# 192 instead of 160 tokens gathered in a product-key expert layer, with the gathers begun in the one-hot stage

## The chip, the cores and the metric

The kernel runs on one core of one Trainium2 chip. The metric is device time in microseconds of one execution, the median of several runs. The core has five engines with a queue each: TensorE (PE, matmuls, with its weight loads as PEld), VectorE (DVE), ScalarE (ACT), GpSimd (POOL) and SyncE (SP), and 16 DMA engines that the queues of SP, ACT and POOL share.

## The reference, cut to what matters

One encoder layer over 512 tokens of width 2048. The first half (gated linear attention and dilated window attention) isn't touched by the change. The second half is a channel mixer that looks up 128 x 128 = 16384 single-neuron experts:

```
qry = (xt @ w_query).reshape(T, 8, 2, 128)
sc = einsum('thcd,hckd->thck', qry, sub_keys)
top_s, top_i = top_k(sc, 16)                  # per token, head and side
cand_s = top_s[:, :, 0, :, None] + top_s[:, :, 1, None, :]
best_s, best_pos = top_k(cand_s, 16)          # 16 experts per token and head
idx, gates = ..., softmax(best_s)
u = expert_down[idx];  act = gelu(einsum('tkd,td->tk', u, x))
out = einsum('tk,tkd->td', gates * act, expert_up[idx])
```

So each token uses 8 x 16 = 128 experts, each with one row of `expert_down` and one of `expert_up` (8 KB each).

## The kernel before, in words

The second half treats two groups of tokens in two ways. 352 tokens are **dense** (`DENSE`, lines 24 to 31): all 16384 experts are computed for them by matmuls, and the gates, zero for the experts that a token doesn't use, are multiplied in. The other 160 are **gathered** (`NG` = `NA` + `NB2` = 128 + 32): for them the rows of the experts used are fetched from DRAM by index and multiplied on VectorE. A batch of 128 tokens lies on the 128 partitions (`xn`), so one slot (a head's k-th expert) takes one indirect DMA of 128 rows, 128 of them for the down rows and 128 for the up rows. The 32 tokens lie four times over the partitions (`xb`), so 32 DMAs serve their 128 slots. Each such row tile, 1 MB, is fetched by POOL's queue (`fetch_rows`, three buffers, two ahead; line 1180), and VectorE does one operation on it: a product with a sum for the down rows (line 1194), a scaled addition for the up rows (line 1209).

The weights of the dense part come as 128 down blocks and 128 up loads of 1 MB on SP's queue. `Stream` splits each into two pieces, each piece into a high half (ScalarE, line 71) and a lo half (VectorE or POOL, line 79, after `add_down`), and each product is three fp32r matmuls (`mm3`, lines 120 to 122), whose moving operand has 352 columns.

The stages in question, each in program order:

- **Query projection** (`Scores`, 8 heads x 4 loads): six matmuls per weight tile, three over the dense and three over the gathered columns. Beside it VectorE and POOL do the top-k of the heads (`TopK`, in pieces that `pieces` hands out).
- **Tail**: 42 steps (`HEAD`) of three matmuls for the first of the `EARLY` = 3 down blocks, with the top-k of the last head for the dense tokens between them.
- **One-hot stage** (88 steps of four dense tokens): VectorE compares indices with an iota (e, line 1118) and multiplies by the gates (w, line 1121); TensorE multiplies the two one-hots into a gate matrix of all experts (line 1146), which goes to DRAM (`gt_d`). Between the steps a filler does the down products of `INSIDE` = 19 more blocks, whose lo pieces are POOL's. The last top-k pieces stand here, and at step 70 the indices of the gathered tokens are made (`gathered_slots`). Activations of the first 8 blocks stay in SBUF (`pre0` to `pre7`), those of 16 more go to DRAM (`pre_d`) by `pre_store`.
- **Dense stage**: two more early blocks, then 16 groups of eight blocks: the down products not yet done, gelu, gates, split (`Weighted`), and 16 up loads. `after` is called once per piece and lets `gather` advance in proportion to the steps. All gathering stands in this stage. The gates come back from DRAM every four blocks (`fetch_gates`, the first two on POOL's queue, ahead of the gathers).

Every engine takes its instructions in the order in which the program writes them; no scheduler reorders them.

## Time and profile before

| | |
|---|---|
| median of 3 runs | 3273.18 us (3270.42 to 3275.17) |
| the profiled execution | 3277.63 us, span 3275.9 us |
| TensorE busy | 3210.5 us, 98% |
| VectorE busy | 2370.4 us, 72% |
| ScalarE, POOL busy | 36%, 28% |
| moved by DMA | 774.37 MB, 236 GB/s over the span |

Busy is the time in which an engine has at least one instruction running. TensorE's matmuls overlap, so its pace is read from the distance of their starts and not from their durations. A row of the timeline gives start, duration, engine, line, operation, operands and shapes. A row of stretches gives, for each engine, its busy time and its number of instructions, then the granted TensorE clock (1.00 is 2.4 GHz), the busy share of the DMA engines and their rate.

### The profile page before, as it was taken

The page shows a single profiled execution, that of the slowest core. Times are in us where ns is not written, and L with a number is a line of the kernel's source. Part 1 is how long each engine was busy: PE and PEld are TensorE (multiplying, and loading weights), DVE is VectorE, ACT ScalarE, POOL GpSimd, SP SyncE. Part 2 cuts the span into 40 slices and gives each one's busy share as a digit, 9 for nine tenths or more (in the row PEclk, how much of TensorE's full clock was granted, in tenths as well). Part 3 has the DMA queues.
Part 4 walks back from the last instruction along what each step waited for, and adds up shares of the span by engine and source line. Part 5 has one row for each costly group of instructions (what it writes and reads, how often), then busy time and mean ns, then how long its engine had stood idle before and what let it go on. Part 6 is the DMA issues. An engine that isn't in the chain of part 4 may idle for free.

```text
span 3275.9 us, 47661 instructions
## 1 busy us (share of the span) xinstructions
PE 3210.5 (98%) x19090; PEld 3012.4 (92%) x19090; DVE 2370.4 (72%) x3754; ACT 1178.4 (36%) x1892; POOL 919.6 (28%) x714
## 2 busy tenths in 40 slices
PE   8999999999999989998999999999999999999999
PEld 6778887878899988988999999999999999999999
DVE  5544445464457779946888888888888888888886
ACT  4334344453323345643333332332332332333332
POOL 3112020201235555501323323223233333233331
PEclk9999999999999999999999999999999999999999
DMA  4222222224322234577898989899889898988996
GB/s 148 81 91 93 75 94 73 96 94 143 131 83 91 80 142 178 187 279 264 331 342 346 348 324 351 327 347 343 339 332 351 316 353 324 356 344 329 356 344 228
DMA packets 157229, 774.37 MB, mean 236 GB/s; under 512 B 13264, under 2 KB 64784, under 8 KB 70672
## 3 DMA queue, kind: packets, MB, share of 16 engines
q1 hardware_dynamic: 99744, 389.31, 33.9%
q0 software_dynamic: 48768, 348.73, 27.0%
q10 hardware_dynamic: 8496, 33.30, 2.6%
q8 instruction: 150, 2.46, 0.3%
q14 instruction: 71, 0.58, 0.0%
HBM read 733.79 MB, written 37.49 MB: 235 GB/s over the span
## 4 chain that ended last, share of the span: by engine, by line
PE 78%; DVE 12%; DMA 5%; issue 2%; ACT 2%; POOL 1%; DVEq 0%; ACTq 0%; SPq 0%; POOLq 0%
PE pj L122 17%; PE pj L120 17%; PE pj L121 17%; PE pa L122 7%; PE pa L120 7%; PE pa L121 7%; DMA wr16x<-in_downT_dram 2%; DVE e L1118 2%; DMA wr4x<-in_upT_dram 2%; DVE w L1121 2%; DVE wl2x L79 1%; PE pa L603 1%; PE pa L544 1%; DVE row L1194 1%; PE pj L1146 1%
## 5 line engine op out<-in xcount | busy, mean ns | idle before, releaser
L79 DVE TENSOR_TENSOR wl2x<-wr4x,wh2x 128x1024 fp32r<-128x1024 f32 x382 | 467.3, 1230 | 350.3 <-ACT wh2x L71 344.4
L122 PE MATMUL pj<-ah,wl2x 128*128 128x352 f32 x2048 | 667.6, 326 | 9.7 <-DVE wl2x L79 9.5
L120 PE MATMUL pj<-ah,wh2x 128*128 128x352 f32 x2048 | 664.3, 324 | 12.3 <-ACT wh2x L71 12.2
L121 PE MATMUL pj<-al,wh2x 128*128 128x352 f32 x2048 | 662.4, 323 | 1.0 <-DVE al L1243 1.0
L122 PE MATMUL pa<-yh,wl8x 128*128 128x352 f32 x2000 | 652.2, 326 | 10.8 <-POOL wl8x L79 8.9
L120 PE MATMUL pa<-yh,wh8x 128*128 128x352 f32 x2000 | 660.2, 330 | 0.6 <-ACT wh8x L71 0.6
L121 PE MATMUL pa<-yl,wh8x 128*128 128x352 f32 x2000 | 645.8, 323 | 0.0
L71 ACT CAST wh2x<-wr4x 128x1024 fp32r<-128x1024 f32 x382 | 396.8, 1048 | 661.0 <-DMA wr4x<-in_upT_dram 384.9
L1180 POOL DMA_INDIRECT row<-in_down_dram,idx x160 | 255.1, 1595 | 678.1 <-DVE ga L1194 674.3
L1180 POOL DMA_INDIRECT row<-in_up_dram,idx x160 | 272.2, 1701 | 579.4 <-DVE xn L1209 432.5
L122 PEld LDWEIGHTS pj<-ah,wl2x 128*128 128x128 f32 x2048 | 386.9, 189 | 18.1 <-DVE wl2x L79 15.7
L120 PEld LDWEIGHTS pj<-ah,wh2x 128*128 128x128 f32 x2048 | 386.5, 189 | 14.9 <-ACT wh2x L71 14.3
L121 PEld LDWEIGHTS pj<-al,wh2x 128*128 128x128 f32 x2048 | 387.8, 189 | 2.1 <-DVE al L1243 1.9
L122 PEld LDWEIGHTS pa<-yh,wl8x 128*128 128x128 f32 x2000 | 374.9, 187 | 13.6 <-POOL wl8x L79 10.4
L120 PEld LDWEIGHTS pa<-yh,wh8x 128*128 128x128 f32 x2000 | 377.2, 189 | 2.0 <-ACT wh8x L71 1.0
L121 PEld LDWEIGHTS pa<-yl,wh8x 128*128 128x128 f32 x2000 | 376.6, 188 | 0.0
L71 ACT CAST wh8x<-wr16x 128x1024 fp32r<-128x1024 f32 x256 | 267.1, 1046 | 200.9 <-DMA wr16x<-in_downT_dram 129.3
L79 DVE TENSOR_TENSOR wl8x<-wr16x,wh8x 128x1024 fp32r<-128x1024 f32 x212 | 258.8, 1223 | 95.4 <-ACT wh8x L71 95.4
L1209 DVE SCALAR_TENSOR_TENSOR xn<-row,ga,xn 128x2048 f32<-128x2048 f32 x127 | 298.0, 2347 | 0.1
L1194 DVE CUSTOM_DVE_ANT_0 row<-row,xn 128x2048 f32<-128x2048 f32 x128 | 292.6, 2286 | 0.0
L120 PE MATMUL pj<-wh2x,xh 128*128 128x512 f32 x704 | 284.1, 404 | 0.0
L121 PE MATMUL pj<-wl2x,xh 128*128 128x512 f32 x704 | 274.7, 390 | 1.2 <-DVE wl2x L79 1.2
(330 smaller groups left out, 4842.6 us busy)
## 6 DMA issues: line engine op xcount, KB each, us to landing
wr16x<-in_downT_dram SPq DMA_DIRECT2D x128, 1024.0 KB, 6.8
wr4x<-in_upT_dram SPq DMA_DIRECT2D x128, 1024.0 KB, 7.5
wr4x<-in_win_dram SPq DMA_DIRECT2D x47, 1024.0 KB, 4.9
gt_d<-gs ACTq DMA_DIRECT2D x11, 2048.0 KB, 7.1
g<-gt_d SPq DMA_DIRECT2D x30, 704.0 KB, 8.8
wr4x<-in_wout_dram SPq DMA_DIRECT2D x16, 1024.0 KB, 5.0
wr8x<-in_wq_dram SPq DMA_DIRECT2D x16, 1024.0 KB, 5.1
xt<-in_xT_dram POOLq DMA_DIRECT2D x4, 1024.0 KB, 6.5
```

The lines of the kernel that those rows point to most:

```text
L71: self.nc.scalar.copy(hi, t)
L79: self.lo_engine[n].tensor_tensor(lo, t, hi.bitcast(F32), op=OP.subtract)
L120: nc.tensor.matmul(out, sh, mh, start=first, stop=False)
L121: nc.tensor.matmul(out, sh, ml, start=False, stop=False)
L122: nc.tensor.matmul(out, sl, mh, start=False, stop=last)
L544: nc.tensor.matmul(sc[u], qt[:, h, t * 128:(t + 1) * 128], kt[:, h, :], start=True, stop=True)
L603: nc.tensor.matmul(oo, vv[:, kb, h * 128:(h + 1) * 128], pt[u][:, kb, :], start=kb == 0, stop=kb == NB - 1)
L1118: nc.vector.tensor_tensor(e, ij[:, :, ts].unsqueeze(2).to_broadcast([128, 2, 128, 4]), io4.unsqueeze(1).to_broadcast([128, 2, 128, 4]), op ...
L1121: nc.vector.tensor_tensor(w[:, 0], e[:, 0].rearrange("p k t -> p t k"), gd[:, ts].unsqueeze(2).to_broadcast([128, 4, 128]), op=OP.mult)
L1180: nc.gpsimd.indirect_dma_start(out=t, out_offset=None, in_=A["up" if up else "down"], in_offset=bass.IndirectOffsetOnAxis(ap=idx[b][:, k:k ...
L1194: nc.vector.tensor_tensor_reduce(t, t, x, 1.0, 0.0, OP.mult, OP.add, g[:, k:k + 1])
L1209: nc.vector.scalar_tensor_tensor(x, t, g[:, k:k + 1], x, op0=OP.mult, op1=OP.add)
```

## The change

- `NB2` goes from 32 to 64: 192 tokens are gathered, 320 are dense. The 64 tokens lie twice over the partitions (`PARTS` = 2), so their slots take 64 DMAs; with the other 128 that is 192 for the down and 192 for the up rows.
- The tail is 122 steps long (`EARLY` = 8). In it the top-k of the gathered tokens comes before that of the dense ones, and all top-k is done there. At step 84 the indices are made and the first two rows fetched. One lo piece of every other early block goes to VectorE.
- The one-hot stage has 80 steps and no top-k; every third step holds one gather (27), while `INSIDE` = 22 blocks fill it.
- All 32 early activations go to DRAM; the eight of each of the first four groups are loaded by SP's queue.
- The dense stage goes on with the gathers where the one-hot stage ended.

```diff
-NB2 = 32
+NB2 = 64
+PARTS = 128 // NB2
...
-    EARLY, INSIDE = 3, 19
+    EARLY, INSIDE = 8, 22
...
-        ws.add(A["downT"][e], 2, () if e >= EARLY + INSIDE else (nc.gpsimd, nc.gpsimd))
+        ws.add(A["downT"][e], 2, () if e >= EARLY + INSIDE else (nc.gpsimd, nc.gpsimd if e >= EARLY or e % 2 else None))
...
             def rest(self):
                 self.packed(sel_h, 256, 64)
-                self.packed(sel_q, 320, 32)
...
                 self.packed(sel_a, DENSE + NB2, 128)
-                self.packed(sel_b, DENSE, 32)
+                self.packed(sel_b, DENSE, NB2)
...
+        gathered = [0]
+
+        def gather_next():
+            gather(gathered[0])
+            gathered[0] += 1
...
         def pre_store():
-            e = len(pre)
-            kept = e < E
-            t = prep.tile([128, DENSE], F32, name=f"pre{e}" if kept else "spill", bufs=1 if kept else 2)
+            t = spill.tile([128, DENSE], F32, name="spill", bufs=2)
             nc.vector.tensor_tensor(t, banks.pop(0), rb2[:, :DENSE], op=OP.mult)
-            if not kept:
-                nc.scalar.dma_start(pre_d[e], t)
+            nc.scalar.dma_start(pre_d[len(pre)], t)
             pre.append(t)
...
-        HEAD = 42
+        HEAD = 16 * EARLY - 6
         for n in range(HEAD):
             next(tail)
             if n == 5:
-                assert len(todo) < 8
+                assert len(todo) < 12
                 pieces(len(todo))
+                scored.gathered()
+            if n == 7:
                 scored.whole()
-            if n in (6, 12, 18, 24):
+                scored.rest()
+            if n >= 9 and n % 6 == 3:
                 pieces(1)
-            if n == 14:
-                scored.rest()
-            if n == 16:
-                scored.gathered()
-            if n == 30:
-                pre_store()
-            if n == 36:
+            if n == 84:
+                gathered_slots()
+                fetch_rows(0)
+                fetch_rows(1)
+            if n == 106:
+                assert not todo
                 flush()
-            if n == 40:
+            if n == 112:
                 turned_sel(0)
                 turned_sel(1)
+                turned_part(sel_h, 256, 64)
+            if banks and n % 16 == 5:
+                pre_store()
...
             one_hots(n + 2)
-            if n % 4 == 1 and n < 64:
-                pieces(1)
-            if n in (20, 36, 52, 68):
-                flush()
-            if n == 38:
-                turned_part(sel_h, 256, 64)
-            if n == 40:
-                turned_part(sel_q, 320, 32)
+            if n % 3 == 1:
+                gather_next()
...
-            if n == 70:
-                gathered_slots()
...
-    total = 32 * (NK // E) - 2 * PRE - 24
+    total = 32 * (NK // E) - 2 * PRE - 10
...
-        while gathered[0] < min(END, max(0, steps[0] - 14) * END // total):
+        while gathered[0] < min(END, done[0] + steps[0] * (END - done[0]) // total):
...
-    fetch_rows(0)
-    fetch_rows(1)
+    av = [Weighted(k) for k in range(E)]
+    for w in av:
+        w.fetch()
     for e in range(EARLY + INSIDE, PRE):
         if e == PRE - 1:
-            av = [Weighted(k, pre[k]) for k in range(E)]
             wait = av[:]
         for n, _ in enumerate(pre_act(pa)):
             if e == PRE - 1 and n % 4 == 3:
                 weigh_next(1)
+            if n % 8 == 5:
+                gather_next()
```

The rest moves definitions ahead of their new first use and lets the top-k tiles live in the pool of the projection.

**VectorE's order in the middle of the one-hot stage.** `e` and `w` are the one-hots, `spill` is an early activation scaled; MAX, MATCH_REPLACE, MAX_INDEX and RECIPROCAL belong to the top-k. Before:

```order
L887 RECIPROCAL smk<-smk 128x1 x2
L1038 TENSOR_TENSOR spill<-pa,rb_6105 128x352
L1118 TENSOR_TENSOR e<-ij,io_10134 128x1024
L1121 TENSOR_TENSOR w<-e,gd 128x512
L816 MAX tv<-sc_9683 128x8 x2
L818 MATCH_REPLACE rp<-tv,sc_9683 128x128 x2
L820 MAX_INDEX ti<-tv,sc_9683 128x8 x2
L822 MAX tv<-rp 128x8 x2
L824 MAX_INDEX ti<-tv,rp 128x8 x2
```

Now, where the first `ISA` row is the product with the gathered row tile and the second reads its sum out:

```order
L1082 TENSOR_TENSOR spill<-pa,rb_6105 128x320
L1162 TENSOR_TENSOR e<-ij,io_10712 128x1024
L1165 TENSOR_TENSOR w<-e,gd 128x512
L1030 ISA row,ga_9891<-row,xb 128x2048
L1030 ISA ga_9891 128x1
```

The top-k pieces are gone from between the one-hots, and gathers of 2048 columns stand there instead.

**POOL's order where the one-hot stage ends.** `wl8x` are lo pieces, `g` the gates from DRAM, `row` the gathered row tiles. Before:

```order
L79 TENSOR_TENSOR wl8x_12452<-wr16x_12271,wh8x_12431 128x1024
L79 TENSOR_TENSOR wl8x_12505<-wr16x_12271,wh8x_12497 128x1024
L1216 DMA g<-gt_d 128x11x128 x2
L1180 DMA row<-in_down_dram,idx_9851 128x2048 x32
L1180 DMA row<-in_down_dram,idx_9850 128x2048 x128
```

Now:

```order
L80 TENSOR_TENSOR wl8x_12914<-wr16x_12749,wh8x_12895 128x1024
L1016 DMA row<-in_down_dram,idx_9887 128x2048
L80 TENSOR_TENSOR wl8x_12970<-wr16x_12749,wh8x_12948 128x1024
L1016 DMA row<-in_down_dram,idx_9887 128x2048
L1209 DMA g<-gt_d 128x10x128 x2
L1016 DMA row<-in_down_dram,idx_9887 128x2048 x35
L1016 DMA row<-in_down_dram,idx_9886 128x2048 x128
```

Row gathers now stand among the lo pieces, and the two gate loads, which came ahead of all gathers, stand between them.

## Rows read from the trace of the kernel before

**Rows 1.** Stretches: length; busy of PE, PEld, DVE, ACT, POOL; clock, DMA share, GB/s.

```profile
1126.00:1166.00 40.00, 37.59 (x236) 36.10 (x235) 21.68 (x74) 14.70 (x29) 26.39 (x18) 1.00 0.29 103
1166.00:1406.00 240.00, 222.22 (x1584) 218.19 (x1584) 225.40 (x439) 137.21 (x238) 117.27 (x58) 0.99 0.48 177
1406.00:1600.00 194.00, 174.99 (x1026) 167.51 (x1026) 126.44 (x162) 64.80 (x92) 31.89 (x21) 0.97 0.78 284
1600.00:3200.00 1600.00, 1593.58 (x9787) 1583.92 (x9786) 1373.28 (x1366) 507.68 (x614) 493.68 (x300) 1.00 0.90 341
3200.00:3276.00 76.00, 71.93 (x446) 71.52 (x444) 46.32 (x47) 19.30 (x22) 6.21 (x5) 0.99 0.62 227
```

**Rows 2.** TensorE's timeline from 2500 us: start, duration, engine, line, operation, operands, shapes.

```profile
2499.71 0.33 PE L122 MATMUL pj<-ah,wl2x 128*128 128x352 f32 x1
...
2503.91 0.32 PE L121 MATMUL pj<-al,wh2x 128*128 128x352 f32 x1
```

**Rows 3.** TensorE's timeline from 850 us.

```profile
849.74 0.39 PE L121 MATMUL pj<-ml,wh2x 128*128 128x512 f32 x1
...
851.78 0.39 PE L121 MATMUL pj<-ml,wh2x 128*128 128x512 f32 x1
```

**Rows 4.** TensorE's timeline from 1118 us.

```profile
1118.02 0.28 PE L121 MATMUL pj<-zl,wh4x 128*128 128x160 f32 x1
1118.13 0.28 PE L122 MATMUL pj<-zh,wl4x 128*128 128x160 f32 x1
```

**Rows 5.** Instructions by line, 1166 to 1406: count, busy us, mean ns, idle before.

```profile
L1118 DVE TENSOR_TENSOR e<-ij,io 128x1024 bf16<-128x1024 bf16 x84 | 103.1, 1227 | 0.0
L1121 DVE TENSOR_TENSOR w<-e,gd 128x512 f32<-128x512 bf16 x85 | 77.4, 910 | 18.9 <-PE pj L1146 10.3
L1038 DVE TENSOR_TENSOR spill<-pa,rb 128x352 f32<-128x352 f32 x13 | 6.7, 517 | 0.0
...
L79 POOL TENSOR_TENSOR wl8x<-wr16x,wh8x 128x1024 fp32r<-128x1024 f32 x34 | 90.5, 2668 | 98.4 <-ACT wh8x L71 85.9 <-PE pa L122 8.8 <-PE pj L1146 3.7
```

**Rows 6.** VectorE's timeline around 1304 us.

```profile
1304.52 2.65 DVE L1121 TENSOR_TENSOR w<-e,gd 128x512 f32<-128x512 bf16 x1
1307.10 2.86 DVE L1118 TENSOR_TENSOR e<-ij,io 128x1024 bf16<-128x1024 bf16 x1
1310.06 0.69 DVE L1121 TENSOR_TENSOR w<-e,gd 128x512 f32<-128x512 bf16 x1
```

**Rows 7.** POOL's timeline at the same time.

```profile
1303.83 5.58 POOL L79 TENSOR_TENSOR wl8x<-wr16x,wh8x 128x1024 fp32r<-128x1024 f32 x2
```

**Rows 8.** Line 1118 over the whole span: duration ns min/median/max, first and last start.

```profile
L1118 DVE TENSOR_TENSOR e<-ij,io x88: 662/686/2905, 1152.4 to 1399.6; 128x1024 bf16<-128x1024 bf16 x88
```

**Rows 9.** Instructions by line, the page's costliest groups.

```profile
L79 DVE TENSOR_TENSOR wl2x<-wr4x,wh2x 128x1024 fp32r<-128x1024 f32 x382 | 467.3, 1230 | 350.3 <-ACT wh2x L71 344.4
...
L1209 DVE SCALAR_TENSOR_TENSOR xn<-row,ga,xn 128x2048 f32<-128x2048 f32 x127 | 298.0, 2347 | 0.1
L1194 DVE CUSTOM_DVE_ANT_0 row<-row,xn 128x2048 f32<-128x2048 f32 x128 | 292.6, 2286 | 0.0
```

**Rows 10.** The page: rate in 40 slices, and the queues.

```profile
GB/s 148 81 91 93 75 94 73 96 94 143 131 83 91 80 142 178 187 279 264 331 342 346 348 324 351 327 347 343 339 332 351 316 353 324 356 344 329 356 344 228
...
q1 hardware_dynamic: 99744, 389.31, 33.9%
q0 software_dynamic: 48768, 348.73, 27.0%
```

**Rows 11.** Two stretches of 20 us.

```profile
2560.00:2580.00 20.00, 20.00 (x125) 20.00 (x124) 16.11 (x15) 6.50 (x9) 4.79 (x4) 1.00 1.01 399
...
3080.00:3100.00 20.00, 20.00 (x126) 20.00 (x125) 16.82 (x17) 6.50 (x9) 6.74 (x4) 1.00 0.99 372
```

**Rows 12.** Who waited for whom, 1406 to 1600: total us, times, longest.

```profile
POOL g L1216 <- DMA pre_d<-spill: 19.6, 1, 19.6
```

**Rows 13.** Line 1180, the row gathers.

```profile
DMA to landing us min/median/max: 6.2/9.1/18.0
```

More of the change, by code (lines that the diff above doesn't have):

```diff
@@ L949, in packed @@
                 if self.h % (2 * per) == 0:
-                    last = self.h == 8 - 2 * per
-                    packed[n, first] = (kp if last else qp).tile([128, 4, NK], F32, name=f"sc{first}",
-                                                                 bufs=2 if n == 128 and not last else 1)
+                    packed[n, first] = qp.tile([128, 4, NK], F32, name=f"sc{first}",
+                                                                 bufs=2)
                 sc = packed[n, first]
@@ L1004, in layer, with fetch_rows, weights_of_slots, gather @@
         qs = slot.tile([128, NB2], F32, name="qs")
-        prep = pool(ctx, "prep", side="right")
+        spill = pool(ctx, "spill", side="right")
+        rows = pool(ctx, "rows", side="right")
+        fetched = {}
+        events = [(up, b, k) for up in range(2) for b in (1, 0) for k in range(n_slots[b] + up)]
+        TURN = sum(n_slots)
+        def fetch_rows(n):
+            if n < len(events):
+                up, b, k = events[n]
+                fetched[n] = t = rows.tile([128, D], F32, name="row", bufs=3)
+                if k == n_slots[b]:
+                    nc.gpsimd.dma_start(t[:NB2 if b else 128, :], (x1g_d, x1b_d)[b])
+                else:
+                    nc.gpsimd.indirect_dma_start(out=t, out_offset=None, in_=A["up" if up else "down"],
+                                                 in_offset=bass.IndirectOffsetOnAxis(ap=idx[b][:, k:k + 1], axis=0))
+        def weights_of_slots():
+            for b in range(2):
+                nc.scalar.activation(ga[b], ga[b], AF.Gelu_apprx_tanh, scale=rg[:, b:b + 1])
+                nc.vector.tensor_tensor(ga[b], ga[b], gate[b], op=OP.mult)
+        def gather(n):
+            fetch_rows(n + 2)
+            up, b, k = events[n]
+            t, x, g = fetched.pop(n), (xn, xb)[b], ga[b]
+            if not up:
+                nc.vector.tensor_tensor_reduce(t, t, x, 1.0, 0.0, OP.mult, OP.add, g[:, k:k + 1])
+            elif k == n_slots[b]:
+                if b:
+                    for c in range(4):
+                        cs = slice(c * 512, c * 512 + 512)
+                        bank = pa()
+                        nc.tensor.matmul(bank[:NB2, :], qs, x[:, cs], start=True, stop=True)
+                        nc.vector.tensor_tensor(t[:NB2, cs], t[:NB2, cs], bank[:NB2, :], op=OP.add)
+                    nc.gpsimd.dma_start(out_b, t[:NB2, :])
+                else:
+                    nc.vector.tensor_tensor(x, x, t, op=OP.add)
+                    nc.gpsimd.dma_start(out_g, x)
+            elif k == 0:
+                nc.vector.tensor_scalar(x, t, g[:, 0:1], None, op0=OP.mult)
+            else:
+                nc.vector.scalar_tensor_tensor(x, t, g[:, k:k + 1], x, op0=OP.mult, op1=OP.add)
+        gathered = [0]
+        def gather_next():
+            gather(gathered[0])
+            gathered[0] += 1
         def act_part(b, q, hi, lo, a):
@@ L1157, in layer @@
     slot2.close()
+    prep = pool(ctx, "prep", side="right")
+    d2 = pool(work, "d2")
     xres = pool(ctx, "xres", side="right")
@@ L1164, in fetch_x1 @@
         nc.sync.dma_start(x1[:, 4 * dc:4 * dc + 4, :], x1_d[:, 4 * dc:4 * dc + 4, :])
-    rows = pool(ctx, "rows", side="right")
-    d2 = pool(work, "d2")
-    fetched = {}
-    events = [(up, b, k) for up in range(2) for b in (1, 0) for k in range(n_slots[b] + up)]
-    TURN = sum(n_slots)
-    def fetch_rows(n):
-        if n < len(events):
-            up, b, k = events[n]
-            fetched[n] = t = rows.tile([128, D], F32, name="row", bufs=3)
-            if k == n_slots[b]:
-                nc.gpsimd.dma_start(t[:NB2 if b else 128, :], (x1g_d, x1b_d)[b])
-            else:
-                nc.gpsimd.indirect_dma_start(out=t, out_offset=None, in_=A["up" if up else "down"],
-                                             in_offset=bass.IndirectOffsetOnAxis(ap=idx[b][:, k:k + 1], axis=0))
-    def weights_of_slots():
-        for b in range(2):
-            nc.scalar.activation(ga[b], ga[b], AF.Gelu_apprx_tanh, scale=rg[:, b:b + 1])
-            nc.vector.tensor_tensor(ga[b], ga[b], gate[b], op=OP.mult)
-    def gather(n):
-        fetch_rows(n + 2)
-        up, b, k = events[n]
-        t, x, g = fetched.pop(n), (xn, xb)[b], ga[b]
-        if not up:
-            nc.vector.tensor_tensor_reduce(t, t, x, 1.0, 0.0, OP.mult, OP.add, g[:, k:k + 1])
-        elif k == n_slots[b]:
-            if b:
-                for c in range(4):
-                    cs = slice(c * 512, c * 512 + 512)
-                    bank = pa()
-                    nc.tensor.matmul(bank[:NB2, :], qs, x[:, cs], start=True, stop=True)
-                    nc.vector.tensor_tensor(t[:NB2, cs], t[:NB2, cs], bank[:NB2, :], op=OP.add)
-                nc.gpsimd.dma_start(out_b, t[:NB2, :])
-            else:
-                nc.vector.tensor_tensor(x, x, t, op=OP.add)
-                nc.gpsimd.dma_start(out_g, x)
-        elif k == 0:
-            nc.vector.tensor_scalar(x, t, g[:, 0:1], None, op0=OP.mult)
-        else:
-            nc.vector.scalar_tensor_tensor(x, t, g[:, k:k + 1], x, op0=OP.mult, op1=OP.add)
     gates = {}
@@ L1245, in layer @@
     pipe = []
-    steps, gathered = [0], [0]
-    total = 32 * (NK // E) - 2 * PRE - 24
+    steps, done = [0], []
+    total = 32 * (NK // E) - 2 * PRE - 10
     END = len(events)
@@ L1274, in layer @@
         fetch_gates(e)
-    av, wait = [], []
+    wait = []
     def weigh_next(n):
@@ L1294, in layer @@
     early = []
+    done.append(gathered[0])
     for sb in range(NK // E):
```

61 lines of the change are left out of this document (27 added, 34 removed).

## The prediction

> **What bounds the kernel now.** I read the table of stretches first. Up to 1126 us the matmuls of the query projection follow one another without a gap [rows 4], and the change touches little before them. Then come three stretches with different limits [rows 1]. In the tail, 1126 to 1166, TensorE has 37.59 of 40 us and the other engines have room. In the one-hot stretch, 1166 to 1406, VectorE has 225.40 of 240 us: it sets the pace, and TensorE idles 18 us. In the dense stretch, 1406 to 3276, TensorE is full again (1593.58 of 1600 us), with VectorE at 86% and the transfers at a share of 0.90. So there the rule is: TensorE first, DMA second, VectorE third, and all three are close. The change takes work from the first and gives it to the second and third.
>
> I then read the spacing of matmuls on TensorE's timeline. With 352 columns 27 starts lie between 2499.71 and 2503.91, 26 steps of 161.5 ns [rows 2]. With 512 columns ten starts lie between 849.74 and 851.78, 226.7 ns each [rows 3]. A column costs (226.7 - 161.5) / 160 = 0.4075 ns, so 320 columns come to 148.5 ns, 13.0 ns less. The gathered part, 160 columns, starts 0.11 us apart [rows 4], more than the 0.083 us that this slope gives. It stands on a floor, and at 192 columns the slope gives 0.096, still below it.
>
> All sums go against the profiled execution, 3277.6 us. The median of the three runs, 3273.2, is 4.4 below it, which I take off at the end. A difference under about 0.2% (7 us) can't be told from none here.
>
> **Query projection: -10 us.** 8 heads x 16 x 2 = 256 groups of six matmuls, three of them over dense columns: 256 x 3 x 13.0 ns = 10.0 us. The three over gathered columns stay on their floor. If they grew by the slope instead, the gain would be 0; the 0.11 us rows speak against that.
>
> **Tail: +36 us.** The first part before the one-hots grows from 42 to 122 steps of three matmuls: 80 x 3 x 148.5 = +35.6 us, 42 x 3 x 13.0 = -1.6 us, and about 2 us for the transposes of the 64 tokens that came later. This work isn't lost: it is taken from what follows. Beside it VectorE gets four more top-k groups. Of its 225 us in the one-hot stretch the one-hots have 103.1 + 77.4 and the spills 6.7 [rows 5]; at most 38 us are left for those groups. VectorE had 21.68 of 40 us in the tail, so it fits into 76. POOL had 26.39 of 40 us; with some six lo pieces more and four decodes it comes to about 70 of 76. That is tight, and its first two row issues now stand behind VectorE's index casts and ahead of lo pieces, so the bound upwards is +46.
>
> **One-hot stretch: +30 us.** VectorE's one-hot operations are short when alone, 0.69 us each (w at 1310.06, the median of e), but w took 2.65 and e 2.86 while POOL formed two lo pieces, 1303.83 to 1309.41 [rows 6 to 8]. The spill, whose input is in PSUM, stays at 0.52 on the mean [rows 5]. So for operations that read SBUF twice the two engines take turns. Check: 84 + 85 one-hot operations at 0.69 are 117 us, but they took 180.5, so 63 us went into waiting for POOL. The rest of POOL's 117.27 us lay beside top-k, spills and idle time.
> The change takes out the top-k that hid POOL and puts in 27 gathers. Now: 77 steps x 2 x 0.69 = 106 us, 27 x 2.29 = 62 us [rows 9], 20 spills at 0.5 = 10 us. POOL's 41 lo pieces at 2.67 us are 109 us, of which the 10 us of spills hide some. That is 277 to 287 us; successive operations overlap by some 70 ns (1307.10 against 1304.52 + 2.65), which gives back about 15, and a few us stay idle as before. I take 270. TensorE needs 326 x 3 x 148.5 ns = 145 us and 640 one-hot passes on the floor of 0.11 = 70 us, 215 in all, which is hidden. Bounds: 235, if a gather doesn't wait for POOL, which no row shows since the two never meet in this trace; 290, if the lo pieces are late too. I stay near the upper end because e and w, both with two SBUF inputs, behave so.
> The Trainium skill, SBUF — State Buffer, section "Who interferes with whom", says that a VectorE instruction with two SBUF inputs and a GpSimd instruction that reads SBUF exclude one another for a whole instruction. By it the gathers take turns as well, and the stretch is 270; without it 235. The trace agrees for e and w (2.86 and 2.65 against 0.69 us); for the gathers no row decides.
>
> **Dense stretch: -85 us.** 30 of 128 down blocks are now done before it instead of 22.
> - TensorE: 98 x 48 + 6144 = 10848 matmuls at 148.5 ns = 1611 us.
> - VectorE: 126.44 + 1373.28 + 46.32 = 1546 us now. Gathers: 165 down and 192 up instead of 160 and 160, 5 x 2.29 + 32 x 2.35 = +87 us. Sixteen lo pieces fewer at 1.23, -20 us. About 640 operations lose 32 columns at no more than 1230 / 1024 = 1.2 ns, some -22 us [rows 9]. That is 1591 us, just under TensorE.
> - DMA: the queues' rows give the price per MB, 0.270 x 3275.9 / 348.73 = 2.54 us on the software queue and 0.339 x 3275.9 / 389.31 = 2.85 on the hardware queue [rows 10]; so 2.66 us a row gather and 2.99 us a weight MB (1.0486 MB each). Check on before: 320 x 2.66 + 232 x 2.99 + 91 for 32 MB of gates, residual and output = 1636, against 0.78 x 194 + 0.90 x 1600 + 0.62 x 76 = 1638 from [rows 1]. Now: 355 rows (two are fetched ahead) 944 us, 224 weight MB 670, and 32 MB of the rest 90, among them 32 loads of early activations instead of 16; on SP's queue eight of them now stand ahead of weight loads once more in each of the first groups, at 0.16 MB each, which that sum holds. Sum 1704 us.
> So **the transfers become the bound**, 6% above TensorE. How full can the 16 engines be kept? Ends: 0.90, what the bulk had while TensorE set the pace, and 1.01, what 2560 to 2580 had [rows 11]. I take 0.97, near the stretches of 0.99 to 1.01: 1704 / 0.97 = 1757 us.
> Added are 28 us: 19 that TensorE idled from 1406 to 1600, 4 at the end, where rows no longer come, and 5 because POOL's two gate loads, which waited 19.6 us for the last store [rows 12], now have 35 row gathers queued behind them. Two rows are already there, so this costs between 0 and 19.6. Sum 1785 against 1870.
>
> Together 3277.6 - 10 + 36 + 30 - 85 = 3248.6, or **3244 us** on the scale of the median.
>
> **The rivals.**
> *Starved transfers, slower (0.30).* Only three row buffers exist. A row lands 9.1 us after its issue (up to 18.0) [rows 13], its operation takes 2.3, so a buffer is bound for 11.4 us at least, or 3.8 us a row with three; before, a row came every 5.8 us (1870 / 320), now one must come every 5.0, with the landing time growing as the engines fill. VectorE takes its instructions in order, so a late row holds back the lo pieces, and then TensorE. At 0.93 the stretch takes 1704 / 0.93 + 28 = 1860, in sum 3324, or 3319. It decides below 0.954, where 1704 / 0.954 + 28 = 1814 eats the 56 us saved. For it: the early steps already had TensorE at 175 of 194 us with a share of 0.78. Against: at 0.99 and 1.01 TensorE had 20.00 of 20 us [rows 11].
> *A rate limit below the engines' own (0.07).* 640 MB move in the stretch (372 rows, 235 weights, 32 rest). No slice of 82 us brought more than 356 GB/s [rows 10]; if that is a ceiling, they take 1798 + 28 = 1826 us, in sum 3290, or 3285, a little slower. But no slice asked for more, and stretches of 20 us ran at 399 and 372 GB/s [rows 11]. The Trainium skill, SBUF — State Buffer, section "A bandwidth-pool intuition that's wrong (but worth ruling out)", gives about 358 GB/s from HBM to one core, by which the time would be 3276; those two stretches contradict it for 20 us.
> *Gathers don't wait for POOL (0.10).* The one-hot stretch stays at 235: 3214, or 3209. For it: POOL's gather issues never lengthen the gathers' own operation (2286 ns mean), but they are no lo pieces.
> *The engines' share isn't the limit (0.05).* If packets overlap more when they queue (1.01 is above one already), TensorE and VectorE decide, 1611 / 0.985 + 25 = 1660: 3124, or 3119.
>
> **How the numbers follow.** My forecast has 0.48, of which 0.38 is faster by over 0.2%, 0.08 within, 0.02 slower. The two faster rivals add 0.15, the starved transfers 0.29 slower and 0.01 within, the rate limit 0.03 within and 0.04 slower: faster 0.53, same 0.12, slower 0.35. The range, 3195 to 3325, leaves out the last rival and the worse half of the starved transfers, about 0.2. Since both signs hold much, the forecast's own range is 3215 to 3275.
>
> **What would show it.** Right: matmuls about 148 ns apart where TensorE isn't held up; the one-hots start near 1190 and end near 1460; gathers in that stretch well over 2.29 us where a lo piece runs; DMA at 0.95 or more from then on, with TensorE near 92% and its waits going back to lo pieces and rows. Wrong: gathers of 2.29 us there; VectorE waiting for rows by hundreds of us with DMA under 0.93; or a DMA share well below 0.95 and TensorE still full.

## The result and the profile after

The changed kernel takes 3313.0 us (median of 4 runs, 3308.3 to 3324.4) where the kernel before, on the same chip, takes 3271.8 (4 runs): ratio 1.0131, 95% interval 1.0103 to 1.0158. It is slower by 41 us where 29 us less were forecast. The profiled execution has a span of 3322.6 us; it is the longest of the four, 11 us above the median.

The table of stretches of the changed kernel, with the columns of [rows 1]: tail, one-hot stretch, and the dense stretch in three pieces (its first 237 us, its bulk, its end).

```profile
core 0: us, PE busy (x) PEld busy (x) DVE busy (x) ACT busy (x) POOL busy (x), PEclk, DMA share, GB/s
1116.00:1190.00 74.00, 62.71 (x381) 60.57 (x380) 63.94 (x266) 24.23 (x55) 56.45 (x43) 0.89 0.43 151
1190.00:1463.00 273.00, 243.09 (x1710) 236.74 (x1709) 252.43 (x232) 129.75 (x201) 164.16 (x72) 0.97 0.72 269
1463.00:1700.00 237.00, 187.04 (x1127) 175.28 (x1127) 177.31 (x216) 69.20 (x99) 61.17 (x40) 0.91 0.88 332
1700.00:3240.00 1540.00, 1438.65 (x9258) 1376.28 (x9258) 1350.24 (x1324) 473.86 (x587) 511.05 (x314) 0.99 0.93 355
3240.00:3322.00 82.00, 75.70 (x497) 72.62 (x495) 57.36 (x57) 23.32 (x28) 11.25 (x8) 1.00 0.73 264
```

The bulk of before had TensorE at 1593.58 of 1600 us with the transfers at 0.90 [rows 1]. Now TensorE has 93%, and the transfers stand at 0.93, VectorE at 88%: no resource is full. The dense stretch takes 237 + 1540 + 82 = 1859 us; the forecast was 1785, and before it took 1870.

High and low parts are the high halves and lo pieces of the split weights. The one-hots' own rows, and the gathers in that stretch (the view of one tile, as [rows 8]):

```profile
L1162 DVE TENSOR_TENSOR e<-ij,io x80: 674/684/2896, 1186.1 to 1460.5; 128x1024 bf16<-128x1024 bf16 x80
...
L1030 DVE CUSTOM_DVE_ANT_0 row<-row,xb x26: 2278/2288/4485, 1209.6 to 1456.1; 128x2048 f32<-128x2048 f32 x26
```

The first one-hot moved from 1152.4 us [rows 8] to 1186.1, the last from 1399.6 to 1460.5. So up to there the change costs 61 us where 56 were forecast, and from there on it gives back 14 (1876.3 to 1862.1 us) where 85 were forecast. The miss lies in the dense stretch.

Matmuls with 320 columns, on TensorE's timeline as [rows 2]; eleven rows between these two are left out:

```profile
2499.78 0.31 PE L122 MATMUL pj<-al,wh2x 128*128 128x320 f32 x1
...
2501.55 0.31 PE L122 MATMUL pj<-al,wh2x 128*128 128x320 f32 x1
```

Twelve steps in 1.77 us are 147.5 ns, where 148.5 was forecast. TensorE does need less; it is held up. Who waits for whom in the bulk (waits, 1700 to 3240; us in total, times, longest):

```profile
ACT wh2x L72 <- DMA wr4x<-in_upT_dram: 305.9, 60, 13.0
ACT wh8x L72 <- DMA wr16x<-in_downT_dram: 150.1, 46, 9.2
...
DVE wl8x L80 <- ACT wh8x L72: 70.8, 45, 5.9
PEld pa L123 <- DVE wl8x L80: 66.2, 117, 2.3
...
PEld pj L123 <- DVE wl2x L80: 56.9, 83, 2.5
...
PE pa L123 <- DVE wl8x L80: 35.1, 59, 2.1
PE pj L123 <- DVE wl2x L80: 33.8, 54, 2.2
...
PE pj L121 <- ACT wh2x L72: 19.7, 11, 3.6
...
DVE xn L1045 <- DMA row<-in_up_dram,idx: 13.8, 12, 5.6
```

TensorE waits for low parts (69 us on its matmul queue) and for high parts (30 us, 10 of them for the down blocks), VectorE for high parts, ScalarE for weights to land; for rows VectorE waits next to nothing. The queue that issues the weight loads waits in its turn for VectorE (the same stretch, SyncE's queue), which closes a loop:

```profile
SPq L60 <- DVE wl2x L80: 628.5, 99, 13.7
SPq L60 <- DVE wl8x L80: 603.0, 94, 9.6
```

And the times from issue to landing there (the DMA issues of the bulk; xcount, KB each, median us):

```profile
wr4x<-in_upT_dram SPq DMA_DIRECT2D x97, 1024.0 KB, 8.0
wr16x<-in_downT_dram SPq DMA_DIRECT2D x96, 1024.0 KB, 8.3
...
row<-in_up_dram,idx POOLq DMA_INDIRECT x186, 9.4
row<-in_down_dram,idx POOLq DMA_INDIRECT x126, 9.1
```

193 weight loads in 1540 us are one per 7.98 us. With two buffers a round takes 15.96 us: 8.15 to land, 7.8 until both low parts are formed and the buffer is asked for again. A hold in which the parts follow at TensorE's pace is one high part (1.05 us), half a load's matmuls (24 x 147.5 ns = 3.54 us) and one low part (1.23 us), 5.8 us. This is an estimate and not a floor: single holds in the trace are as short as 4.9 us. By it a load comes every (8.15 + 5.8) / 2 = 7.0 us, against 48 x 147.5 ns = 7.08 us that TensorE needs for one. The loop has next to no slack: what makes a load land later or a low part wait behind a gather should show in the time, which the runs below test. Before, the same wait was there and cost nothing (waits of the kernel before, 1600 to 3200):

```profile
ACT wh2x L71 <- DMA wr4x<-in_upT_dram: 324.9, 69, 9.4
...
PEld pj L122 <- DVE wl2x L79: 6.3, 8, 1.5
```

There a load was needed every 48 x 161.5 ns = 7.75 us, and landed after 7.5 to 7.7 us; by the same estimate one could come every 6.9.

A second loss follows the waits. TensorE stood idle from 1485 to 1495 us, waiting for a high part, and the granted clock was at its lower level, 1.2 GHz, from 1487 to 1504 (stretches, as in the table):

```profile
1485.00:1495.00 10.00, 0.22 (x2) 0.00 (x0) 2.70 (x3) 1.10 (x3) 0.95 (x1) 0.61 1.02 421
1495.00:1505.00 10.00, 6.78 (x24) 5.69 (x25) 7.47 (x11) 3.57 (x7) 0.95 (x1) 0.54 0.67 220
```

At the mean clocks of the table, 0.91 and 0.99, the dense stretch loses some 0.09 x 237 = 21 and 0.01 x 1540 = 15 us of TensorE's full pace. No run separates this from the waits ahead of it.

### The profile page after: what moved, and what is told of

It is laid out like the page before. It is cut to its first block, busy times and chain, and to the rows that moved or that the text cites. A ratio compares the mean times of both kernels' runs of the same rounds, so it can differ in the third digit from the quotient of the medians.

```text
span 3322.6 us, 47706 instructions
## 1 busy us (share of the span) xinstructions
PE 3107.3 (94%) x18966; PEld 2847.4 (86%) x18966; DVE 2485.0 (75%) x3822; ACT 1153.1 (35%) x1866; POOL 1047.6 (32%) x787
## 4 chain that ended last, share of the span: by engine, by line
PE 40%; DVE 19%; issue 18%; DMA 13%; POOL 6%; ACT 3%; DVEq 0%; POOLq 0%; SPq 0%; ACTq 0%
PE pj L123 10%; PE pj L121 10%; PE pj L122 10%; POOL row L1016 6%; DMA row<-in_up_dram,idx 5%; DMA wr4x<-in_upT_dram 4%; DVE row L1030 3%; DVE e L1162 3%; DMA wr16x<-in_downT_dram 2%; DVE xn L1045 2%; DVE wl2x L80 2%; DVE w L1165 2%; DVE wl8x L80 1%; DVE xb L1045 1%; PE pa L604 1%
## 5 line engine op out<-in xcount | busy, mean ns | idle before, releaser
L123 PE MATMUL pj<-ah,wl2x 128*128 128x320 f32 x2048 | 654.7, 320 | 50.4 <-DVE wl2x L80 48.6
L121 PE MATMUL pj<-ah,wh2x 128*128 128x320 f32 x2048 | 645.5, 315 | 51.7 <-ACT wh2x L72 51.5
L123 PE MATMUL pa<-yh,wl8x 128*128 128x320 f32 x1920 | 612.6, 319 | 40.4 <-DVE wl8x L80 36.2
L122 PE MATMUL pj<-al,wh2x 128*128 128x320 f32 x2048 | 643.3, 314 | 2.5 <-DVE al L1236 2.5
L121 PE MATMUL pa<-yh,wh8x 128*128 128x320 f32 x1920 | 607.2, 316 | 12.8 <-ACT wh8x L72 12.7
L122 PE MATMUL pa<-yl,wh8x 128*128 128x320 f32 x1920 | 598.6, 312 | 0.0
L1016 POOL DMA_INDIRECT row<-in_up_dram,idx x192 | 317.1, 1651 | 624.7 <-DVE xn L1045 362.9
L1016 POOL DMA_INDIRECT row<-in_down_dram,idx x192 | 303.3, 1580 | 583.7 <-DVE ga L1030 563.8
L121 PEld LDWEIGHTS pa<-yh,wh8x 128*128 128x128 f32 x1920 | 366.5, 191 | 16.3 <-ACT wh8x L72 16.1
L122 PEld LDWEIGHTS pa<-yl,wh8x 128*128 128x128 f32 x1920 | 365.9, 191 | 0.0
```

The lines of the kernel that those rows point to most:

```text
L121: nc.tensor.matmul(out, sh, mh, start=first, stop=False)
L122: nc.tensor.matmul(out, sh, ml, start=False, stop=False)
L123: nc.tensor.matmul(out, sl, mh, start=False, stop=last)
L1016: nc.gpsimd.indirect_dma_start(out=t, out_offset=None, in_=A["up" if up else "down"], in_offset=bass.IndirectOffsetOnAxis(ap=idx[b][:, k:k ...
```

## The experiments

Four theories were on the table. **A**: too few rows under way (the rival of the prediction). **B**: VectorE, in order and 88% busy, delivers low parts late. **C**: the engines can't be filled further. **D**: the loop of two weight buffers. All ratios are against the kernel before. The runs are told in groups, not in their order. They were made on several chips, on which the kernel before took 3270 to 3276 us, so a difference of some 10 us between two of the runs can't be told from none; "by the ratios" sets each run against the kernel before on its own chip.

### Rows and their buffers

**rows4**

```diff
-fetched[n] = t = rows.tile([128, D], F32, name="row", bufs=3)
+fetched[n] = t = rows.tile([128, D], F32, name="row", bufs=4)
-fetch_rows(n + 2)
+fetch_rows(n + 3)
```

> Changed kernel with a fourth row buffer and rows fetched three ahead instead of two. Theory A (too few rows under way: in the trace of the changed kernel the engines' share from 1700 to 3240 is 0.89 while one row gather is under way, 0.95 with two and 0.98 with three): that stretch goes from 0.93 to about 0.97, 1540 x 0.93 / 0.97 = 1476 us, and the time from 3313 to about 3250 (3230 to 3275). Theory B (VectorE, in order and 88% busy, delivers low parts late; rows don't matter): within 10 us of 3313. Theory C (0.93 to 0.95 is all that this mix of transfers can give): within 10 us of 3313, share unchanged, with rows landing later after their issue.

Measured: 3307.5 us, ratio 1.0089 (1.0064 to 1.0114), 5 us less than the changed kernel (14 by the ratios). VectorE's waits for rows are gone from the list, and the rest stands. Its bulk in the table of stretches:

```profile
1700.00:3225.00 1525.00, 1428.09 (x9212) 1366.62 (x9211) 1341.89 (x1316) 471.89 (x583) 504.18 (x312) 0.99 0.93 357
```

Its waits there:

```profile
ACT wh2x L72 <- DMA wr4x<-in_upT_dram: 329.7, 63, 13.0
ACT wh8x L72 <- DMA wr16x<-in_downT_dram: 153.2, 51, 8.4
...
PEld pa L123 <- DVE wl8x L80: 59.2, 105, 1.6
```

Rows that come earlier alone change little: theory A, as a cause by itself, falls.

**rows2**

```diff
-fetched[n] = t = rows.tile([128, D], F32, name="row", bufs=3)
+fetched[n] = t = rows.tile([128, D], F32, name="row", bufs=2)
-fetch_rows(n + 2)
+fetch_rows(n + 1)
```

> Changed kernel with two row buffers and rows fetched one ahead instead of three and two. Theory A: the share falls to that of one row under way or none, 0.80 to 0.89, and the dense stretch becomes 1704 / 0.85 + 28 = about 2030 us, so about 3480 (3420 to 3600). Theory B: late rows hold VectorE's queue only now and then, 3330 to 3380. Theory C: the engines stay as full as they were, within 30 us of 3313.

Measured: 3622.4 us, ratio 1.1061 (1.1028 to 1.1094). That is above even theory A's case. The sum of the prediction's rival bites here: with two buffers a row takes at least (8.4 to land + 2.3) / 2 = 5.35 us, times 355 rows 1900 us, more than the 1859 of three buffers; the dense stretch took 3626.7 - 1463 = 2164. VectorE waits for rows by hundreds of us (1700 to 3540):

```profile
DVE row L1030 <- DMA row<-in_down_dram,idx: 156.8, 71, 5.3
...
DVE xn L1045 <- DMA row<-in_up_dram,idx: 147.8, 68, 7.7
```

So beside two weight buffers three row buffers are enough and two are not; the changed kernel stands on the right side of this edge.

**half_rows and half_ops**

```diff
+row = [rows.tile([128, D], F32, name=f"row{k}") for k in range(3)]
...
-indirect_dma_start(out=t, out_offset=None, in_=A["up" if up else "down"],
+indirect_dma_start(out=t[:, :D // 2], out_offset=None, in_=A["up" if up else "down"].rearrange("r (h c) -> (r h) c", h=2),
```

> Each row gather brings only 1,024 of the 2,048 numbers of a row (the other half of the buffer stays zero, so half of each dot product and of each weighted sum is left out); VectorE's operations keep their full width. The transfers lose 355 x 2.66 / 2 = 472 us of engine time, 1704 to 1232. Theories A and C (transfers are the bound): the dense stretch falls to TensorE's 1611 us and some 40 to 60 idle, time about 3100 (3080 to 3140). Theory B (VectorE is late because it is full): the dense stretch stays above 1800, time 3260 to 3313.

```diff
-nc.vector.tensor_tensor_reduce(t, t, x, 1.0, 0.0, OP.mult, OP.add, g[:, k:k + 1])
+nc.vector.tensor_tensor_reduce(t[:, :D // 2], t[:, :D // 2], x[:, :D // 2], 1.0, 0.0, OP.mult, OP.add, g[:, k:k + 1])
```

(and the weighted sum of the up rows likewise)

> Whole rows are fetched, but VectorE's multiply-and-sum and its weighted sum take only 1,024 of 2,048 columns (half of each dot product and weighted sum is left out). VectorE loses about 357 x 1.15 = 410 us, the transfers nothing. Theory B: the dense stretch goes towards TensorE's 1611 us, time 3120 to 3180. Theory A: a buffer is free 1.15 us sooner of some 11.5, so rows are asked for sooner: 3250 to 3290. Theory C: within 10 us of 3313 but for the one-hot stretch, which may give back up to 30 us (26 gathers of 3.3 us there).

Measured: 3198.7 us (0.9767, 0.9745 to 0.9790) and 3201.2 us (0.9775, 0.9750 to 0.9800). A, B and C missed both: taking about a quarter off the transfers or off VectorE's work gives 112 to 114 us, and none of them has that. That the two are alike is in part chance: with half the operations the last one-hot starts at 1431.1 us instead of 1460.5, so 29 us come from the one-hot stretch, and the dense stretch takes 1762 us, where with half rows it takes 1732. The bulk with half rows:

```profile
1700.00:3115.00 1415.00, 1381.11 (x9113) 1336.91 (x9112) 1322.99 (x1295) 463.82 (x571) 525.57 (x309) 1.00 0.77 266
```

The bulk with half operations:

```profile
1670.00:3115.00 1445.00, 1387.19 (x9199) 1364.63 (x9198) 1031.68 (x1316) 472.86 (x583) 386.52 (x312) 0.98 0.96 376
```

With half the operations the engines ran at 0.96, so 0.93 is no ceiling: theory C falls. With half the rows VectorE was as busy as ever (93%) and TensorE ran at 98%, so VectorE's load alone is no bound either. A loop in which a landing and a low part follow each other explains both: with half the rows a load lands after 6.0 us instead of 8.15, and with half the operations, where it lands after 9.0, a round takes 2 x 1445 / 192 = 15.05 us, which leaves 6.0 instead of 7.8 for the hold.

### The loop of the weights

**raw3**

```diff
+ws.more, ws.first, ws.raw = pool(work, "more"), len(ws.loaded), 3
+ws.load(len(ws.loaded) + 1)
 gates = {}
...
+if self.more and (len(self.loaded) - self.first) % 3 == 0:
+    t = self.more.tile([128, a, b], F32, name=f"{self.name}r{a}x{b}", tag=f"{self.name}r", bufs=1)
```

> Changed kernel with a third buffer for raw weights in the dense stretch, so a weight load is issued one load earlier. Theory D (the loop of two weight buffers sets the pace: a load lands 8.2 us after its issue on the median, is needed some 10.7 us after the low part that frees its buffer, and that low part stands behind gathers in VectorE's queue): ScalarE's waits for weights to land (456 us from 1700 to 3240) and TensorE's waits for low parts both fall, the stretch 1700 to 3240 comes to about 1460 us, time 3220 to 3250. Theory B (VectorE, 88% busy and in order, delivers low parts late whatever the weights do): weights land earlier, but the time stays within 12 us of 3313. Theory C (0.93 to 0.95 of the engines is all this mix gives): within 10 us, share unchanged.

Measured: 3253.6 us (4 runs, 3251.1 to 3258.7), ratio 0.9943 (0.9923 to 0.9964): 59 us less than the changed kernel, and faster than the one before. First part and bulk of the dense stretch:

```profile
1463.00:1700.00 237.00, 201.72 (x1270) 189.90 (x1268) 199.25 (x241) 78.48 (x116) 68.92 (x44) 0.95 0.97 371
1700.00:3175.00 1475.00, 1397.68 (x9116) 1345.96 (x9116) 1328.61 (x1298) 466.53 (x572) 519.26 (x309) 0.99 0.96 365
```

The waits of that bulk (1700 to 3175):

```profile
ACT wh2x L76 <- PE pj L126: 300.0, 116, 8.6
...
ACT wh2x L76 <- DMA wr4x<-in_upT_dram: 42.3, 9, 9.7
...
DVE xn L1049 <- DMA row<-in_up_dram,idx: 27.7, 21, 4.5
DVE row L1034 <- DMA row<-in_down_dram,idx: 21.1, 24, 3.1
...
DVE xb L1049 <- DMA row<-in_up_dram,idx: 9.1, 11, 2.3
```

and TensorE's own:

```profile
PE pj L127 <- DVE wl2x L84: 39.4, 51, 3.2
PE pa L127 <- DVE wl8x L84: 32.7, 48, 3.0
...
PE pj L125 <- ACT wh2x L76: 1.9, 2, 1.6
```

ScalarE's 306 us of waiting for up weights became 42; it now waits for TensorE, 300 us, which means that it is ahead. Loads land later than with two buffers (8.9 and 9.1 us on the median) and it doesn't matter. Theory D holds, within 4 us of the time that it gave (3220 to 3250), but not in all that it said: of TensorE's waits those for high parts went (30 to 2 us), those for low parts stayed (69 to 72). The dense stretch took 3256.9 - 1463 = 1794 us. What is late next is the row: 58 us of waits in VectorE's queue.

**ahead2**

```diff
+more = self.more and (n - self.first) % 4 == 0
...
-hi, lo = ws.next()
+hi, lo = ws.next(2)
```

> Changed kernel with a fourth buffer each for high and low parts in the dense stretch, and each piece split two pieces ahead of its use instead of one. Theory B: a low part has 3.6 us more until TensorE needs it, more than a gather's 2.35 us; TensorE's waits for low parts (about 190 us on the matmul and weight-load queues, 1700 to 3240) mostly go, time 3220 to 3260. Theory D: splitting earlier frees raw buffers no sooner relative to the load that follows, while the parts of a late load are still late: 3290 to 3313. Theory C: within 10 us of 3313.

Measured: 3301.0 us, ratio 1.0084 (1.0057 to 1.0112), 12 us less than the changed kernel, as theory D had it (3290 to 3313). ScalarE still waits 487 us for weights; TensorE waits less for low parts of weights (44 and 22 us on the weight-load queue instead of 66 and 57), but now for the activations' low parts (33 us) that VectorE forms later. Splitting earlier moves the wait.

**raw3_rows4 and trim**

raw3 and rows4 together; for their room the split activations lose one buffer each.

```diff
-self.hi = d2.tile([128, DENSE], F32R, name="ah", bufs=E + 2)
+self.hi = d2.tile([128, DENSE], F32R, name="ah", bufs=E + 1)
-self.lo = d2.tile([128, DENSE], F32R, name="al", bufs=E + 1)
+self.lo = d2.tile([128, DENSE], F32R, name="al", bufs=E)
```

> Three weight buffers and four row buffers with rows fetched three ahead; to make room, one buffer each less of the split activations (9 high, 8 low). With three weight buffers VectorE waited 58 us for rows from 1700 to 3175. If the transfers are at their ceiling there (share 0.96, 0.98 with three rows under way), these waits go but the stretch gains at most 0.02 x 1475 = 30 us: 3225 to 3250. If VectorE's waits for rows alone hold it: 3195 to 3225. If nothing is held by rows: within 6 us of 3254.

> Changed kernel with one buffer less each for the high and low parts of the activations (9 and 8), the edit that made room for the fourth row buffer beside the third weight buffer. If it has no part in the gain: within 8 us of 3313. If fewer buffers change when VectorE forms these parts, and that is part of the gain: 3285 or less.

Measured: 3191.2 us (4 runs, 3190.8 to 3191.5), ratio 0.9738 (0.9716 to 0.9759), better than any of the cases set down, which took 0.98 for the engines' ceiling and the waits for rows for all that a row can hold up. The trimmed buffers alone: 3318.4 us, 1.0124 (1.0098 to 1.0149), no part in it. The fourth row buffer, worth 5 us (14 by the ratios) beside two weight buffers, is worth 62 beside three.

First part and bulk of raw3_rows4's dense stretch:

```profile
1463.00:1700.00 237.00, 205.18 (x1289) 193.16 (x1287) 203.86 (x252) 80.24 (x118) 72.77 (x45) 0.96 1.00 382
1700.00:3107.00 1407.00, 1375.92 (x9076) 1333.28 (x9077) 1317.45 (x1285) 463.50 (x565) 528.10 (x308) 1.00 0.97 380
```

TensorE's waits for low parts in that bulk:

```profile
PE pj L127 <- DVE wl2x L84: 16.9, 35, 1.2
...
PE pa L127 <- DVE wl8x L84: 12.0, 33, 1.3
```

So the third weight buffer took away the waits for high parts, and the fourth row buffer, beside it, more than half of those for low parts (72 to 29 us); alone it left them at 65. The two loops meet in VectorE's queue, where a late row can hold back a low part, and a late low part the next load. Together the two edits bring the engines to 1.00 and 0.97, TensorE to 98%, and the dense stretch to 1726 us.

**raw3_half_rows**: the two edits named, together.

> Three weight buffers, and each gather brings 1,024 of a row's 2,048 numbers (the other half of the buffer is zero, so half of each dot product and weighted sum is left out). 472 us of the transfers' 1704 go. If transfers bound the dense stretch of the kernel with three weight buffers: TensorE's 1611 us and some 60 idle remain, the time falls by about 110 us or more, 3100 to 3145. If VectorE's load bounds it: 3190 to 3240, no better than half rows with two weight buffers (3199).

Measured: 3191.4 us, 0.9738 (0.9711 to 0.9766), the time of raw3_rows4 to 0.2 us, with the engines at 0.77 in the bulk. That the transfers bound it, the first case, falls; the time lies at the lower edge of the second, in which VectorE's load does. Its bulk:

```profile
1700.00:3107.00 1407.00, 1375.19 (x9078) 1331.84 (x9079) 1317.94 (x1285) 463.73 (x565) 527.10 (x308) 1.00 0.77 267
```

So with rows in time a quarter of the transfers is worth nothing: they mattered through the landing times of loops without slack. What holds the rest (9076 x 147.5 ns are 1339 of these 1407 us) is open. VectorE is busy for 94% of them, and TensorE's waits left are for its low parts; no run halves VectorE's operations beside the deeper buffers.

### The start of the dense stretch, and the one-hot stretch

**start**

```diff
-for e in range(0, 8, 4):
-    fetch_gates(e)
...
+if e < PRE - 1 and n in (6, 14):
+    fetch_gates(n // 8 * 4)
+if n % 2 == 0 and late_loads:
+    late_loads.pop(0)()
```

> Changed kernel with only the first steps of the dense stretch rearranged: the two loads of gate values are issued on POOL within the next activation block instead of ahead of its row gathers, and the eight loads of early activations go out one every two steps on SP's queue instead of all at once ahead of weight loads. In the changed kernel TensorE lost 50 of 237 us from 1463 to 1700, 18 of them in one wait for a weight load at 1480. If that burst is the cause, the stretch gives back 20 to 35 us: 3278 to 3293. If the stretch is simply short of transfer time (0.88 to 1.0 of the engines), the loss moves to the next steps: within 8 us of 3313.

Measured: 3309.9 us, ratio 1.0110 (1.0086 to 1.0133): 3 us (7 by the ratios). The 18 us of the expectation are ScalarE's wait; TensorE's longest idle time there was 10.5 us. TensorE gets 196.42 instead of 187.04 us in the first 237, and loses it again later. The burst isn't the cause; with deeper buffers TensorE had 205.18 us there, with the burst in place.

**nb32**: the changed order, with the number of tokens of before.

```diff
-NB2 = 64
+NB2 = 32
...
+self.packed(sel_q, 320, 32)
```

> The changed order (top-k in the tail, gathers from the one-hot stretch on, 32 early activations in DRAM) with 160 gathered tokens instead of 192. Worked out from the kernel before: TensorE's work stays that of before, the tail grows by about 40 us, the one-hot stretch to about 295 us of VectorE's work, the dense stretch shrinks by 8 blocks x 48 x 161.5 ns = 62 us, so about 3300 (3280 to 3320) if the order costs what it adds to the one-hot stretch. If the longer time comes from the 32 more tokens (64 minus 32 rows more to fetch) alone, the time stays within 8 us of 3275.

Measured: 3333.0 us, ratio 1.0188 (1.0168 to 1.0207). So the order alone costs 62 us, more than was set down, and the 32 tokens more give back 20. Its one-hot stretch and the bulk of its dense stretch:

```profile
1200.00:1504.00 304.00, 275.72 (x1876) 270.08 (x1876) 277.13 (x260) 144.38 (x233) 180.17 (x84) 0.97 0.71 262
...
1700.00:3252.00 1552.00, 1542.01 (x9458) 1532.51 (x9457) 1275.82 (x1269) 495.22 (x598) 430.67 (x262) 1.00 0.86 322
```

With 352 columns TensorE has 99% of the bulk and two weight buffers suffice. The run has 64 row gathers fewer too, and its share is 0.86, so it doesn't separate the columns from the rows; that the 320 columns use up the slack (7.08 against 7.75 us a load) is argued from the sum.

**lov, raw3_lov and raw3_lov_g2**

```diff
-ws.add(A["downT"][e], 2, () if e >= EARLY + INSIDE else (nc.gpsimd, nc.gpsimd if e >= EARLY or e % 2 else None))
+ws.add(A["downT"][e], 2, () if e >= EARLY else (nc.gpsimd, nc.gpsimd if e % 2 else None))
```

and, for the last one,

```diff
-if n % 3 == 1:
+if n % 2 == 1:
     gather_next()
```

> The kernel with three weight buffers (3254 us), and the low parts of the one-hot stretch formed by VectorE instead of POOL. If VectorE's operations with two SBUF inputs take turns with POOL's low parts, each of some 43 low parts costs VectorE up to 2.87 us of waiting now and 1.23 us of work then: one-hots 106 + gathers 27 x 2.29 = 62 + spills 10 + 43 x 1.23 = 53, 231 us less overlaps; TensorE, busy 243 us, decides, and the stretch goes from 275 to about 245 us, gathers to 2.28 us each, time 3217 to 3232. If they don't take turns, VectorE gets 53 us more to do in a stretch in which it is full: 3295 to 3310.

> As the one before (low parts of the one-hot stretch on VectorE, three weight buffers), and a gather on every second one-hot step instead of every third: 39 or 40 rows are done there instead of 27. If the transfers bound the dense stretch with three weight buffers (share 0.96), it loses 13 x 2.66 / 0.96 = 36 us, and the one-hot stretch grows by no more than 13 x 2.29 = 30 us, less what VectorE idles there: 10 to 30 us faster than the one before, 3195 to 3215. If TensorE or VectorE bound the dense stretch, it loses at most 13 x 2.35 = 30 us of VectorE's work there and gains as much before: within 8 us of the one before.

> Changed kernel (two weight buffers, three row buffers) with the low parts of the one-hot stretch formed by VectorE. If the turns cost this stretch 30 us whatever follows: one-hots end near 1430, time about 3313 - 32 = 3281 (3270 to 3290). If the dense stretch is held by something that runs on at its own pace, as the transfers, and takes the time back: 3300 to 3313.

Measured: raw3_lov 3219.8 us, 0.9824 (0.9802 to 0.9845), 34 us under raw3; raw3_lov_g2 3232.9, 0.9867 (0.9844 to 0.9891); lov 3302.1, 1.0079 (1.0063 to 1.0095). In raw3_lov no one-hot and no gather is lengthened any more (the view of one tile):

```profile
L1166 DVE TENSOR_TENSOR e<-ij,io x80: 680/685/695, 1188.8 to 1431.3; 128x1024 bf16<-128x1024 bf16 x80
...
L1034 DVE CUSTOM_DVE_ANT_0 row<-row,xb x26: 2283/2286/2289, 1206.2 to 1428.0; 128x2048 f32<-128x2048 f32 x26
```

VectorE takes over 44 low parts and its last one-hot starts 29 us sooner: the turns are shown. The Trainium skill, SBUF — State Buffer, section "Who interferes with whom", states this exclusion; the gathers' longest time, 4485 ns with POOL's low parts and 2289 without, agrees. In lov the stretch ends as early, but the time falls by 11 us alone, as the second case had it: from the last one-hot to the end it takes 1869 us instead of 1862. More gathers in the one-hot stretch (raw3_lov_g2) gain nothing: in the profiled executions it grows by 32 us and what follows shrinks by 29, and on the medians the kernel is 13 us slower than raw3_lov, which neither case set down.

**raw3_rows4_lov**: all three.

> Three weight buffers, four row buffers and the low parts of the one-hot stretch on VectorE together. If the losses are separate: 3191 - 33 = 3158 (3150 to 3168), 3.5% under the kernel before. If the transfers, at a share of 1.00 in the first 237 us of the dense stretch, take some of it back: 3168 to 3185.

Measured: 3164.7 us (5 runs, 3163.3 to 3167.8), ratio 0.9663 (0.9650 to 0.9677): 111 us under the kernel before, 148 under the changed one. Its one-hot stretch, and the first part and bulk of its dense stretch:

```profile
1190.00:1435.00 245.00, 233.70 (x1710) 228.72 (x1710) 220.26 (x278) 132.48 (x203) 37.25 (x26) 1.00 0.80 298
1435.00:1672.00 237.00, 205.71 (x1281) 193.72 (x1279) 203.15 (x250) 78.61 (x116) 70.75 (x45) 0.95 1.00 380
1672.00:3081.00 1409.00, 1377.08 (x9084) 1334.09 (x9082) 1318.85 (x1285) 465.36 (x569) 534.27 (x308) 1.00 0.98 381
```

The gains add but for 7 us.

## Why the prediction was wrong

**Query projection and tail: right within 8 us.** Together +26 was forecast; the first one-hot starts 33.7 us later than in [rows 8]. In the tail the granted clock was 0.89 over 74 us, some 8 us of TensorE's pace, which the step didn't have; before, it was 1.00 [rows 1]. The 320-column spacing is 147.5 ns, where the step had 148.5.

**One-hot stretch: right.** +30 was forecast, and from the first to the last one-hot it takes 274.4 us instead of 247.2. The gathers take turns with POOL's low parts, as the step assumed from e and w [rows 6 to 8]: 3.21 us on the mean, up to 4.49, against 2.29 alone. The rival in which they don't wait falls.

**TensorE, VectorE and transfers of the dense stretch: right as sums.** 10848 matmuls at 147.5 ns are 1600 us where 1611 were forecast. 1704 us of transfers were forecast; 0.88 x 237 + 0.93 x 1540 + 0.73 x 82 are 1701. VectorE's 1591 came out as 177 + 1350 + 57 = 1585.

**The step that failed.** 3313 lies inside the stated range (3195 to 3325) and outside the forecast's own (3215 to 3275), on the other side of the kernel before. The step that failed is the question "How full can the 16 engines be kept?" and the answer "I take 0.97". It took a property of the engines, seen in two stretches of 20 us [rows 11], for one of the kernel. The engines can do it: with one more buffer for weights and one for rows they stand at 1.00 and 0.97, and the dense stretch takes 1726 us, less than the 1785 forecast. As the change leaves the buffers they are held at 0.88 in the first 237 us and 0.93 after, by the loop of two weight buffers in the main: with a third the stretch takes 1794 us instead of 1859. The forecast needed both loops to have slack, and only that of the rows was worked out, in the rival. It also had nothing for the clock that falls when TensorE is held up, up to some 36 us of its pace here.

**The rival "Starved transfers" gave the right time from half the reason.** At 0.93 it forecast a dense stretch of 1860 and a time of 3319; measured were 1859 and 3313. The 0.93 was worked out from no row, so that it was met is luck. And it put the cause down to three row buffers. A fourth alone gives 5 us (14 by the ratios); a third weight buffer alone gives 59. The loop that it left out needs, by the estimate above, 7.0 us a load where TensorE asks for one every 7.08, while the one it named needs 3.8 us a row where one is wanted every 5.0. VectorE's order does pass the delay on, as the rival said: the fourth row buffer is worth 62 us once the weights have slack.

**The rate limit below the engines' own** is refuted: 382 GB/s over 237 us and 380 over 1407. The figure of about 358 GB/s in the Trainium skill, SBUF — State Buffer, section "A bandwidth-pool intuition that's wrong (but worth ruling out)", is exceeded by 6% for 1.4 ms; the section has it as half of a memory stack's 716, and here one core ran.

**The 28 us added for starts and ends** were too few with the buffers as they are. In the first 237 us TensorE had 187 us, and holding back the gate loads and early activations, which the step blamed, gave 3 us in all.

## What to carry to other kernels

When a change lets one engine go faster, work out for every ring of buffers that feeds it what a round takes (landing and a hold at the new pace, over the number of buffers) and set it against the new rate: a wait that costs nothing before, as ScalarE's 325 us for weights here, tells where to look for the end of the slack. Two rings that meet in one in-order queue are tested together, since a buffer more in one alone can look worth little (5 to 14 us) and be worth 62 beside the other. An operation of POOL that VectorE has to take turns with (2.87 us for 1.23 of VectorE's own work) cost time here once gathers took the place of the top-k beside it.

## What was not expected of the hardware

Beside three weight buffers, half the rows' bytes and a fourth row buffer gave the same bulk to the microsecond, 1407 us, at shares of 0.77 and 0.97: here the share tells nothing of the time. That the 16 engines carry 380 GB/s at a share of 0.97 for 1.4 ms with row gathers and weight loads mixed was not expected either; the kernel before showed 399 for 20 us [rows 11], but at most 375 over 40 us from 1600 to 3200.
